# Layer A of a hybrid trunk: longer planned distances in recurrence and merge, four buffers for keys and queries, one decay matrix, f32 gates from the normed tiles, late modulation

## The chip, the cores and the metric

The kernel runs on one core of one Trainium2 chip. Its engines work side by side, each in its own order: TensorE (PE; PEld is its weight load), VectorE (DVE), ScalarE (ACT), GpSimd (POOL) and SyncE (SP), whose queue issues all DMAs here. The metric is the device time of one execution in microseconds, the median of several runs; lower is better.

## The reference

Two layers over 1024 tokens of width 1024, all in f32. Layer A is a gated delta rule with 8 query/key heads and 16 value heads of width 128, layer B an attention with 16 heads of width 64. Each takes `h = rmsnorm(x) * (1 + scale) + shift` and adds `gate * y`; shift, scale and gate come from one conditioning vector times `ada_w`. Layer A, cut to what matters:

```python
proj = h @ w_in                               # q, k, v | z | b, a
qkv = silu(causal_depthwise_conv(qkv, conv_w))
q, k = l2norm(q) * 128**-0.5, l2norm(k)
beta, g = sigmoid(b), -exp(A_log) * softplus(a + dt_bias)
g = cumsum(g)                                 # within a chunk
decay = exp(where(lower, g[:, None] - g[None, :], -inf))
L = where(strict, (beta k) @ k.T * decay, 0); T = inverse(I + L)
u, w = T @ (beta v), T @ (beta k exp(g))
# chunk after chunk:
v_new = u - w @ state
o = (q exp(g)) @ state + (q @ k.T * decay) @ v_new
state = state * exp(g_last) + (k exp(g_last - g)).T @ v_new
o = rmsnorm(o) * silu(z); y = o @ w_out
```

## The kernel before, in words

Large products run as three f32r matmuls over a high and a low part of each operand (`mm3`, L129 issues all matmuls); small ones run in f32. Layer A treats the sequence in two halves of 512 tokens and 8 groups per half (one key head with its two value heads): 16 groups, each with 4 chunks of 128 tokens.

TensorE's order is written out by a planner, `Flow`. Each strand of work is a generator; a step issues some instructions, and its `yield n` says how many planned TensorE nanoseconds must pass before its next step. The planner always takes the ready strand of the best priority; `fill_a` (the projections and then the output projection) has the worst, so its matmuls fill the planned distances. `pst` and `acc_bank` take a PSUM bank out of a ring, `free(bank, n)` plans its return. The distances (`Y_...`, `R_...`, `LAT`) set an order only: at run time TensorE takes its list in order and waits where data is late. The other engines' orders come from the scheduler of the framework, which also places every semaphore.

The strands, per group: `proj_all` projects k, q, two v tiles and z and runs the convolution (ACT, POOL halo copies, three DVE steps of L764). `prepk` makes a decay matrix `d1`, turns k into tokens (`to_tokens`, evicted by ACT, L923) and makes `L` (`lm`). `invert_blocks` inverts 16x16 diagonal blocks on DVE, passing them through DRAM; `LAT` is the planned time from its start to the merge. `invert_merge` builds the full inverse `r` with small matmuls. `prepv` turns v into tokens, `prep2` makes a second decay matrix `d2`, `qd` (q times the decay, on POOL, L950) and the attention matrix `am`. `chain` is the recurrence. For each chunk it uses bank `ch` for k·state (columns 0:256) and `r`·`xp` (columns 256:512), and bank `co` for the output (columns 0:256) and the state's update:

```python
mm(p1[:, 0:256], kf[:, c], st)                            # ch
xp = p1 * weg + uv              # DVE, L978, one head at a time
yield Y_C0
mm(p1[:, 256 + j*P : ...], r[:, j*CPH + c], xp[:, j*P : ...])
vn = copy(p1[:, 256:512])       # ACT, L991
ve = p1[:, 256:512] * ex        # DVE, L992
yield Y_C1
mm(p2, qd, st); mm(p2, am, vn)                            # co
mm(p2[:, 256:512], ktok, ve); st = st * ex + p2           # L1011
yield Y_C2
```

`finish` norms, transposes and stores a group's output. `gates` makes beta and the decays once per half from an own `mm3` tile over 128 columns of which 32 are used. `start_norm` norms the first half and makes the first modulation columns; `next_norm` norms the second half during the first and stores it in DRAM; `ada_all` makes the remaining modulation rows in 16 strips of 256 columns (`ada_strip`, DVE). Layer B follows and is not touched.

Of the kernel before, what the change touches and what calls it, by code (L numbers as in the profile page):

```python
# [15 lines left out]
P = 128  # L16
D = 1024
# [20 lines left out]
Y_PK = 1200  # L38
# [4 lines left out]
Y_P2 = 4000  # L43
Y_MQ = 2500
Y_MR = 3000
Y_M0 = 1900
Y_M1 = 2000
Y_M2 = 2000
Y_M3 = 2000
Y_C0 = 2200  # L50
Y_C1 = 1700
Y_C2 = 2000
Y_F0 = 9000
Y_F1 = 800
Y_F2 = 2550
# [14 lines left out]
LAT = 36000  # L70
# [15 lines left out]
ADP = 2000  # L86
R_AD = 600
R_OA = 1150
# [95 lines left out]
def tile_trunk(  # L184
# [74 lines left out]
    def ada_strip(alloc, palloc, layer, col, width, wtag, atag, btag, ahead, pace):  # L259
# [38 lines left out]
        else:  # L298
# [3 lines left out]
            flow.free(ps, R_AD)  # L302
# [207 lines left out]
    with ExitStack() as sa:  # L510
# [9 lines left out]
        KQ, ZG = 3, 2  # L520
# [4 lines left out]
        neg_a = at([P, 16], "neg_a")  # L525
        xid = at([P, 8, 16], "xid", 1, BF16)
# [18 lines left out]
        def start_norm():  # L545
            xsT = [at([P, HALF], n, b) for n, b in (("k", KQ), ("k", KQ), ("k", KQ), ("q", 2), ("q", 2))]
            xsT += [at([P, HALF], "ktok", 3) for _ in range(3)]
            for t in range(CPH):
                xt = at([P, D], *(("vtok", 3), ("qd", 2))[t // 2])
                nc.sync.dma_start(xt, x[t * P : (t + 1) * P, :])  # L550
                for d in norm_tile(xt, at([P, D], "ogt", 1), lambda k, p, t=t: nc.scalar.copy(
                    xsT[k][:, t * P : (t + 1) * P], p)):
                    flow.t += d
# [11 lines left out]
            for n in range(2):  # L565
                ps = banks[n]
                acc = at([P, D], "d2", 2)
# [15 lines left out]
                if n == 0:  # L583
                    nc.sync.dma_start(bcol, ada_bc)
                    nc.sync.dma_start(norm_c, norm_col)
                    wload()
                    wload()
# [4 lines left out]
            )  # L592
            for k in range(KT):
# [12 lines left out]
            nc.sync.dma_start(dt_b, a_dt.broadcast_to([P, 16]))  # L606
            nc.sync.dma_start(neg_a, a_log.broadcast_to([P, 16]))
# [3 lines left out]
        def norm_tile(xt, jk, evac):  # L611
            rs = rms_rows(xt, jk, at)
            nc.vector.tensor_scalar(xt, xt, rs, None, op0=ALU.mult)
            yield Y_NN
            for k0 in range(0, KT, 4):
# [7 lines left out]
                flow.free(ps, R_N)  # L623
                yield 500

        def next_norm():
            yield from hold(lambda: done["kqv"] >= 2)
            for t in range(CPH):
                tok = CPH * P + t * P
                xt = at([P, D], "nx", 1)  # L630
                if t == 0:
                    nc.vector.tensor_copy(xt[:, 0:KT], ts[0]["gt"]["ngc"][:, 0, 0:KT])
                nc.sync.dma_start(xt, x[tok : tok + P, :])
                yield 4000
                hf = at([P, KT, P], "nh", 1)

                def evac(k, p):
                    nc.vector.tensor_scalar(
                        hf[:, k], p, gcol[0][:, k : k + 1], scol[0][:, k : k + 1],
                        op0=ALU.mult, op1=ALU.add,  # L640
                    )

                yield from norm_tile(xt, hf.rearrange("p k t -> p (k t)"), evac)
                yield 3000
                nc.sync.dma_start(
                    h1_d[:, :, t * P : (t + 1) * P].rearrange("k p t -> p k t"), hf
                )
            done["norm"] = 1

# [10 lines left out]
        def gates(h, gt):  # L660
            wba_h, wba_l, wba_r = (v.rearrange("p (k f) -> p k f", f=P) for v in wtile(D))
            nc.gpsimd.memset(wba_r, 0.0)
            nc.sync.dma_start(wba_r[:, :, 0:32], wa_ba)
            split(wba_h, wba_l, wba_r)
            yield 4000
# [3 lines left out]
            rows = at([P, HALF], "cv_y", 2)[0:32]  # L669
            nc.scalar.copy(rows, ps[0:32])  # L670
            flow.free(ps, R_AD)
            yield 2500
            pc = yield from pst("tr", 2)
            for c in range(CPH):
                tr_(
                    pc[:, c * 32 : c * 32 + 32], rows[:, c * P : (c + 1) * P], ident[0:32, 0:32]
                )
            pv = pc[:, 0 : CPH * 32].rearrange("p (c n) -> p c n", n=32)
# [7 lines left out]
            flow.free(pc, R_N)  # L686
# [18 lines left out]
            nc.scalar.activation(ex, ex, AF.Exp)  # L705
            ngc = at([P, CPH, 16], "g_ngc", 2)
# [12 lines left out]
            gt.update(col=col, ex=ex, ngc=ngc, beta=beta, g_d=g_d)  # L719
# [54 lines left out]
        def proj_all():  # L774
            for i in range(2 * NG):
                h, g = divmod(i, NG)
                if g == 0:
# [11 lines left out]
                    gt = {}  # L789
                    flow.add(gates(h, gt), 1, HC)  # L790
# [6 lines left out]
                yield from hold(lambda: done["prep2"] >= i - 1)  # L797
                t["q"] = qf = at([P, CPH, P], "q", 2)
# [53 lines left out]
        def decay(t, name):  # L852
# [6 lines left out]
            dv = at([P, 2 * CPH, P], name, 2)  # L859
            low = name == "d1"  # L860
            nc.gpsimd.affine_select(
                out=dv, in_=gb.rearrange("p j (c t) -> p (j c) t", t=P),
                compare_op=ALU.is_gt if low else ALU.is_ge, fill=BIG if low else -BIG, base=0,
                pattern=[[0, 2 * CPH], [-1 if low else 1, P]], channel_multiplier=1 if low else -1,
            )
            bias = t["gt"]["col" if low else "ngc"]
            yield Y_DG
            for j in range(2):
                for c in range(CPH):
# [4 lines left out]
                        dv[:, u], dv[:, u], AF.Exp, scale=-1.0 if low else 1.0, bias=bias[:, c, hd : hd + 1]  # L874
                    )
            return gb, dv

        def prepk(t):
            g, gt, kf = t["g"], t["gt"], t["k"]
            _, d1v = yield from decay(t, "d1")  # L880
            yield Y_PK
            t["ktok"] = ktok = at([P, CPH, P], "ktok", 3)
            t["ss"] = ss = at([P, 2, CPH], "gss", 3)
# [3 lines left out]
            nc.vector.tensor_scalar(rk, ss[:, 0], EPS, None, op0=ALU.add)  # L887
            nc.gpsimd.tensor_tensor(rk, rk, mhalf[:, 0:CPH], op=ALU.pow)
            rkb = bc(rk, 2, 2)
            t["un"] = un = at([P, CPH, 2], "un", 3)  # L890
            t["wn"] = wn = at([P, CPH, 2], "wn", 2)
            t["weg"] = weg = at([P, CPH, 2], "weg", 3)
            nc.vector.tensor_tensor(un, gt["beta"][:, :, 2 * g : 2 * g + 2], rkb, op=ALU.mult)
            nc.vector.tensor_tensor(wn, un, rkb, op=ALU.mult)
            nc.vector.scalar_tensor_tensor(
                weg, wn, -1.0, gt["ex"][:, 1, :, 2 * g : 2 * g + 2], op0=ALU.mult, op1=ALU.mult
            )
            t["lm"] = d1v
# [27 lines left out]
        def prepv(t):  # L926
# [4 lines left out]
            for j in range(2):  # L931
                yield Y_PT
                yield from to_tokens(vt[:, j], vtok[:, :, j], None)
# [4 lines left out]
            for c in range(CPH):  # L938
                nc.gpsimd.tensor_tensor(vtok[:, c], vtok[:, c], bc(t["un"][:, c], 2, P), op=ALU.mult)
# [920 lines left out]
```

## Time and profile before

| | us |
|---|---|
| median of 3 runs | 2041.61 (2041.05 to 2041.88) |
| the profiled execution's own time | 2033.73 |
| its span, first to last instruction | 2032.0 |
| PE busy | 1846.4 (91%) |
| PE weight loads | 1539.1 (76%) |
| DVE busy | 1375.5 (68%) |
| ACT busy | 1035.2 (51%) |
| POOL busy | 483.0 (24%) |

Busy time is a union over the span; a wait row names the instruction that waited, what released it, the total, the number of times and the longest. Layer A's projections and recurrence fill the span to about 1100 us, its output projection goes to about 1300, and layer B takes the rest.

### The profile page before, as it was taken

The page shows a single profiled execution, that of the slowest core. Times are in us where ns is not written, and L with a number is a line of the kernel's source. Part 1 is how long each engine was busy: PE and PEld are TensorE (multiplying, and loading weights), DVE is VectorE, ACT ScalarE, POOL GpSimd, SP SyncE. Part 2 cuts the span into 40 slices and gives each one's busy share as a digit, 9 for nine tenths or more (in the row PEclk, how much of TensorE's full clock was granted, in tenths as well). Part 3 has the DMA queues.
Part 4 walks back from the last instruction along what each step waited for, and adds up shares of the span by engine and source line. Part 5 has one row for each costly group of instructions (what it writes and reads, how often), then busy time and mean ns, then how long its engine had stood idle before and what let it go on. Part 6 is the DMA issues. An engine that isn't in the chain of part 4 may idle for free. (4 is left out here: it accounts for less than half of the span.)

```text
span 2032.0 us, 36238 instructions
## 1 busy us (share of the span) xinstructions
PE 1846.4 (91%) x12940; PEld 1539.1 (76%) x12940; DVE 1375.5 (68%) x3319; ACT 1035.2 (51%) x2684; POOL 483.0 (24%) x518
## 2 busy tenths in 40 slices
PE   4878899998998989999989789999999999999898
PEld 3766677777776777777777567789889889889676
DVE  5788888787878566766656467456666666656764
ACT  4555466555545445555444344255655655655631
POOL 2140232221213021222101223331231231331222
PEclk6999899999999999999999899999999999999999
DMA  6686676766656455454469988020110220211523
GB/s 248 229 258 226 219 240 208 227 214 223 187 173 172 127 160 160 155 163 134 134 225 311 328 299 285 23 64 22 63 63 17 68 63 16 65 56 42 167 85 96
DMA packets 235781, 315.72 MB, mean 155 GB/s; under 512 B 103176, under 2 KB 155936, under 8 KB 235600
## 3 DMA queue, kind: packets, MB, share of 16 engines
q1 hardware_dynamic: 235600, 313.41, 47.6%
q8 instruction: 102, 1.67, 0.3%
q14 instruction: 79, 0.65, 0.1%
HBM read 231.67 MB, written 81.67 MB: 154 GB/s over the span
## 5 line engine op out<-in xcount | busy, mean ns | idle before, releaser
L129 PE MATMUL mm<-ht_h,whi 128*128 128x512 f32 x784 | 352.4, 450 | 7.2 <-DVE olo L301 5.6
L129 PE MATMUL mm<-ht_l,whi 128*128 128x512 f32 x784 | 317.5, 405 | 3.9 <-DVE ht_l L601 3.9
L129 PE MATMUL mm<-ht_h,wlo 128*128 128x512 f32 x784 | 318.0, 406 | 1.8 <-POOL wlo L328 1.8
L129 PE MATMUL mm<-whi,h_h 128*128 128x384 f32 x512 | 187.0, 365 | 0.9 <-DVE kn L1449 0.9
L129 PEld LDWEIGHTS mm<-ht_h,whi 128*128 128x128 f32 x784 | 154.6, 197 | 40.1 <-DVE olo L301 6.5
L129 PEld LDWEIGHTS mm<-ht_h,wlo 128*128 128x128 f32 x784 | 153.4, 196 | 37.8 <-POOL wlo L328 2.2
L129 PEld LDWEIGHTS mm<-ht_l,whi 128*128 128x128 f32 x784 | 155.0, 198 | 31.0 <-DVE ht_l L601 5.2
L764 DVE SCALAR_TENSOR_TENSOR cv_y<-cv_t,conv_h,cv_y 128x512 f32<-128x512 f32 x192 | 147.6, 769 | 43.0 <-ACT cv_y L756 40.8
L129 PE MATMUL mm<-whi,h_l 128*128 128x384 f32 x512 | 173.0, 338 | 0.0
L129 PE MATMUL mm<-wlo,h_h 128*128 128x384 f32 x512 | 172.7, 337 | 0.0
L1600 DVE TENSOR_TENSOR ptl<-pt,pth 128x512 fp32r<-128x512 f32 x192 | 106.3, 555 | 93.9 <-ACT pth L1599 92.2
L1599 ACT CAST pth<-pt 128x512 fp32r<-128x512 f32 x192 | 91.1, 476 | 140.0 <-PE pt L133 139.2
L1443 POOL TENSOR_TENSOR rs<-ss,mhalf 128x4 f32<-128x4 f32 x64 | 64.5, 1007 | 332.4 <-DVE ss L1441 326.7
L328 DVE TENSOR_TENSOR wlo<-ht_h,whi 128x512 fp32r<-128x512 f32 x124 | 91.1, 775 | 59.7 <-ACT whi L325 54.7
L1564 ACT ACTIVATE lg<-lg,mx 128x896 f32<-128x896 f32 (+7 forms) x128 | 99.5, 777 | 55.4 <-DVE mx L1556 49.7
L325 ACT CAST whi<-ht_h 128x512 fp32r<-128x512 f32 x124 | 70.7, 618 | 95.8 <-PE mm L129 35.3
L129 PE MATMUL mm<-h_h,whi 128*128 128x512 f32 x240 | 99.9, 416 | 0.7 <-DVE wlo L1699 0.3
L129 PEld LDWEIGHTS mm<-whi,h_h 128*128 128x128 f32 x512 | 97.8, 191 | 3.5 <-ACT v L1445 1.2
L129 PEld LDWEIGHTS mm<-wlo,h_h 128*128 128x128 f32 x512 | 97.4, 190 | 2.0
L133 PE MATMUL pt<-ident,lg 128*128 128x128 f32 (+1 forms) x584 | 95.6, 272 | 2.4 <-ACT lg L1564 2.4
L325 ACT CAST whi<-wlo 128x512 fp32r<-128x512 f32 (+1 forms) x108 | 62.5, 625 | 67.2 <-DMA wlo<-in_wa_c_dram 30.9
L129 PEld LDWEIGHTS mm<-whi,h_l 128*128 128x128 f32 x512 | 96.6, 189 | 0.0
(366 smaller groups left out, 4702.0 us busy)
## 6 DMA issues: line engine op xcount, KB each, us to landing
ht_h<-in_wa_o_dram SPq DMA_DIRECT2D x62, 512.0 KB
wc<-whi SPq DMA_DIRECT2D x45, 512.0 KB
wc<-wlo SPq DMA_DIRECT2D x45, 512.0 KB
wlo<-wc SPq DMA_DIRECT2D x45, 512.0 KB
whi<-wc SPq DMA_DIRECT2D x45, 512.0 KB
wlo<-in_wa_c_dram SPq DMA_DIRECT2D x35, 512.0 KB
oraw<-in_ada_w_dram SPq DMA_DIRECT2D x128, 128.0 KB
gb<-g_d SPq DMA_DIRECT2D x32, 512.0 KB
```

The lines of the kernel that those rows point to most:

```text
L129: self.nc.tensor.matmul(out, lhsT, rhs, start=start, stop=stop)
L133: self.nc.tensor.transpose(out, src, ident)
L325: nc.scalar.copy(hi, src)
L328: (lo_eng or nc.gpsimd).tensor_tensor(lo, src, hi.bitcast(F32), op=ALU.subtract)
L764: nc.vector.scalar_tensor_tensor(y, raw[:, j : j + HALF], w[:, j : j + 1], y, op0=ALU.mult, op1=ALU.add)
L1443: nc.gpsimd.tensor_tensor(rs, ss, mhalf[:, 0:4], op=ALU.pow)
L1564: nc.scalar.activation(lg, lg, AF.Exp, scale=-1.0, bias=mx[:, hh : hh + 1], accum_out=sums[:, tt : tt + 1],)
L1599: nc.scalar.copy(ph_[:, cs], pp[:, cs])
L1600: nc.vector.tensor_tensor(pl_[:, cs], pp[:, cs], ph_[:, cs].bitcast(F32), op=ALU.subtract)
```

## The change

All of it is in layer A.

- Distances: `Y_C0` 2200 to 2700, `Y_C1` 1700 to 2200, `Y_C2` 2000 to 1700, a new `Y_C3` of 1300 ahead of the state's update; merge steps 500 longer each; `LAT` 36000 to 40000.
- `k` has 4 buffers instead of 3 and `q` 4 instead of 2; `q` no longer waits for `prep2`.
- One decay matrix `d2` serves both uses; its upper triangle feeds `L` transposed, so the merge's products are written the other way round. `d1`'s exponentials, `qd`, and the POOL scaling of v go.
- In `chain` the product with `st` takes plain `q`, is written into `ch`, and is scaled on ACT into `qe`; DVE adds `qe` to the output. `vn` is scaled by `wn` in two ACT steps. The v tokens are scaled in their ACT eviction.
- The gates come from f32 products of the normed tiles with 32 columns, inside `start_norm` and `next_norm`.
- `ada_all` starts after the sixth key projection and runs 8 strips of 512 columns in the tiles of `next_norm`.
- `finish` splits and stores one head at a time out of single buffers.

Core of the diff:

```diff
-Y_PK = 1200
+Y_PK = 1000
-Y_P2 = 4000
-Y_MQ = 2500
+Y_P2 = 3000
+Y_MQ = 3000
-Y_M0 = 1900
-Y_M1 = 2000
+Y_M0 = 2400
+Y_M1 = 2500
...
-Y_C0 = 2200
-Y_C1 = 1700
-Y_C2 = 2000
+Y_C0 = 2700
+Y_C1 = 2200
+Y_C2 = 1700
+Y_C3 = 1300
...
-Y_F1 = 800
-Y_F2 = 2550
+Y_F1 = 900
+Y_F2 = 1600
-LAT = 36000
+LAT = 40000
-ADP = 2000
+ADP = 3500
+AD0 = 5
+R_AS = 2500
...
             nc.vector.tensor_copy(b, ps[0:1, 0:width])
-            flow.free(ps, R_AD)
+            flow.free(ps, R_AS)
...
-        KQ, ZG = 3, 2
+        KQ, ZG = 4, 2
...
         def start_norm():
...
+                for t in range(CPH):
+                    mm(
+                        pc[:, t * 32 : t * 32 + 32], xk[:, t * P : (t + 1) * P], wba[:, k],
+                        start=k == 0 and t == 0, stop=k == KT - 1 and t == CPH - 1,
+                    )
                 nc.vector.tensor_tensor(ht_l[:, k], xk, ht_h[:, k].bitcast(F32), op=ALU.subtract)
+            flow.add(gates(0, gts[0], pc[:, 0 : CPH * 32].rearrange("p (c n) -> p c n", n=32), pc), 1, HC)
...
         def next_norm():
...
+                def part(k0):
+                    yield 2000
+                    ps = yield from pst("tr", 2)
+                    for k in range(4):
+                        mm(ps[:, 0:32], hf[0][:, k], wba[:, k0 + k], start=k == 0, stop=k == 3)
...
-        def gates(h, gt):
-            wba_h, wba_l, wba_r = (v.rearrange("p (k f) -> p k f", f=P) for v in wtile(D))
-            nc.gpsimd.memset(wba_r, 0.0)
-            nc.sync.dma_start(wba_r[:, :, 0:32], wa_ba)
-            split(wba_h, wba_l, wba_r)
-            yield 4000
-            ps = yield from acc_bank()
-            for k in range(KT):
-                mm3(ps, wba_h[:, k], wba_l[:, k], ht_h[:, k], ht_l[:, k], k == 0, k == KT - 1)
...
+        def gates(h, gt, pv, bank=None):
...
-                yield from hold(lambda: done["prep2"] >= i - 1)
-                t["q"] = qf = at([P, CPH, P], "q", 2)
+                t["q"] = qf = at([P, CPH, P], "q", KQ)
...
         def prepk(t):
-            _, d1v = yield from decay(t, "d1")
+            t["d2"] = yield from decay(t)
...
+            t["lm"] = lm = at([P, 2 * CPH, P], "d1", 2)
...
                     nc.vector.scalar_tensor_tensor(
-                        d1v[:, u], mq[:, c * P : (c + 1) * P], wn[:, c, j : j + 1], d1v[:, u],
+                        lm[:, u], mq[:, c * P : (c + 1) * P], wn[:, c, j : j + 1], t["d2"][:, u],
...
         def prepv(t):
...
+                for c in (c0, c0 + 1):
+                    o = 2 * (c - c0) * P
+                    nc.scalar.activation(
+                        vtok[:, c].rearrange("p j f -> p (j f)"), tr[:, o : o + 2 * P], AF.Copy,
+                        scale=t["irk"][:, c : c + 1],
+                    )
...
-            for c in range(CPH):
-                nc.gpsimd.tensor_tensor(vtok[:, c], vtok[:, c], bc(t["un"][:, c], 2, P), op=ALU.mult)
...
         def prep2(t):
-            gb, d2 = yield from decay(t, "d2")
-            t["am"] = am = d2.rearrange("p (j c) t -> p j c t", c=CPH)
-            t["qd"] = qd = at([P, 2, CPH, P], "qd", 2)
-            for j in range(2):
-                yield 2 * Y_DX
-                nc.scalar.activation(gb[:, j], gb[:, j], AF.Exp)
-                nc.gpsimd.tensor_tensor(
-                    qd[:, j], qf, gb[:, j].rearrange("p (c t) -> p c t", t=P), op=ALU.mult
-                )
+            t["am"] = am = t["d2"].rearrange("p (j c) t -> p j c t", c=CPH)
...
         def chain(t):
...
-                            xt[:, sl], p1[:, sl], weg[:, c, j : j + 1], uv[:, c, j],
+                            xt[:, sl], p1[:, sl], neg[:, c, 2 * g + j : 2 * g + j + 1], uv[:, c, j],
...
-                nc.scalar.copy(vn, p1[:, 256:512])
+                for j in range(2):
+                    nc.scalar.activation(
+                        vn[:, j * P : (j + 1) * P], p1[:, 256 + j * P : 256 + (j + 1) * P], AF.Copy,
+                        scale=wn[:, c, j : j + 1],
+                    )
                 nc.vector.tensor_tensor(
                     ve, p1[:, 256:512].rearrange("p (j f) -> p j f", f=P),
-                    bc(ex[:, 0, c, 2 * g : 2 * g + 2], 2, P), op=ALU.mult,
+                    bc(wex[:, c], 2, P), op=ALU.mult,
                 )
-                flow.free(p1, R_C)
+                if not first:
+                    mm(p1[:, 0:256], qf[:, c], st)
+                    qe = at([P, 2 * P], "qe", 2)
+                    for j in range(2):
+                        sl = slice(j * P, (j + 1) * P)
+                        nc.scalar.activation(
+                            qe[:, sl], p1[:, sl], AF.Copy, scale=ex[:, 1, c, 2 * g + j : 2 * g + j + 1]
+                        )
+                flow.free(p1, R_C + 1000)
                 yield Y_C1
                 p2 = yield from pst("co", 1)
                 for j in range(2):
                     sl = slice(j * P, (j + 1) * P)
-                    if not first:
-                        mm(p2[:, sl], qd[:, j, c], st[:, sl], start=True, stop=False)
-                    mm(p2[:, sl], am[:, j, c], vn[:, sl], start=first, stop=True)
+                    mm(p2[:, sl], am[:, j, c], vn[:, sl])
+                yield Y_C3
                 mm(p2[:, 256:512], ktok[:, c], ve.rearrange("p j f -> p (j f)"))
...
+                oc = og[:, c].rearrange("p j f -> p (j f)")
+                if first:
+                    nc.scalar.copy(oc, p2[:, 0:256])
+                else:
+                    nc.vector.tensor_tensor(oc, p2[:, 0:256], qe, op=ALU.add)
                 for j in range(2):
                     jk = at([P, P], "sqt", 1, BF16)
-                    nc.scalar.activation(
-                        jk, p2[:, j * P : (j + 1) * P], AF.Square, accum_out=so[:, c, j : j + 1]
-                    )
-                nc.scalar.copy(og[:, c].rearrange("p j f -> p (j f)"), p2[:, 0:256])
+                    nc.scalar.activation(jk, og[:, c, j], AF.Square, accum_out=so[:, c, j : j + 1])
...
         def finish(t, og, so):
...
+                ogh, ogl = at([P, HALF], "ogh", 1, F32R), at([P, HALF], "ogl", 1, F32R)
+                split(ogh, ogl, ogt, lo_eng=nc.vector)
+                yield Y_F2
+                for v, d in ((ogh, og_d), (ogl, ogl_d)):
+                    nc.sync.dma_start(d[2 * g + j, :, h * HALF : (h + 1) * HALF], v.bitcast(F32))
...
         def ada_all():
-            yield from hold(lambda: done["gates"] == 1)
+            yield from hold(lambda: done["kp"] >= AD0 + 1)
...
             for l, cl in strips:
-                for w0 in (0, 256):
-                    yield from ada_strip(
-                        xt_, acc_bank, l, cl + w0, 256, ("oraw", 3), ("ohi", 4), ("olo", 4), 1, ADP
-                    )
+                yield from ada_strip(
+                    al, acc_bank, l, cl, 512, ("nx", 2), ("nh", 2), ("nh", 2), 1, ADP
+                )
```

More of the change, by code (lines that the diff above doesn't have):

```diff
@@ L592, in start_norm @@
             )
+            pc = yield from pst("tr", 2)
             for k in range(KT):
@@ L623, in norm_tile, with xload @@
                 flow.free(ps, R_N)
+                if part is not None:
+                    yield from part(k0)
                 yield 500
+        gts = [{}, {}]
         def next_norm():
             yield from hold(lambda: done["kqv"] >= 2)
-            for t in range(CPH):
[L629 to L633, printed above, removed]
-                yield 4000
-                hf = at([P, KT, P], "nh", 1)
+            xts = []
+            def xload(t):
+                tok = CPH * P + t * P
+                xts.append(at([P, D], "nx", 2))
+                if t < 2:
+                    nc.vector.tensor_copy(xts[t][:, 0:KT], ts[0]["gt"]["ngc"][:, 0, 0:KT])
+                nc.sync.dma_start(xts[t], x[tok : tok + P, :])
+            xload(0)
+            yield 6000
+            for t in range(CPH):
+                xt = xts[t]
+                if t < CPH - 1:
+                    xload(t + 1)
+                hf = []
@@ L644, in next_norm @@
+                yield from norm_tile(xt, None, evac, part)
                 yield 3000
-                nc.sync.dma_start(
-                    h1_d[:, :, t * P : (t + 1) * P].rearrange("k p t -> p k t"), hf
-                )
             done["norm"] = 1
+            flow.add(gates(1, gts[1], gin), 1, HC)
         def load_norm():
@@ L685, in gates @@
             nc.scalar.activation(e, e, AF.Exp, scale=-1.0)
-            flow.free(pc, R_N)
+            if bank is not None:
+                flow.free(bank, R_N)
             nc.vector.tensor_scalar(beta, beta, 1.0, None, op0=ALU.add)
@@ L788, in proj_all @@
                         load_norm()
-                    gt = {}
-                    flow.add(gates(h, gt), 1, HC)
+                    gt = gts[h]
                 t = dict(h=h, g=g, gt=gt)
@@ L930, in prepv @@
             vtok = at([P, CPH, 2, P], "vtok", 3)
-            for j in range(2):
+            for c0 in range(0, CPH, 2):
                 yield Y_PT
-                yield from to_tokens(vt[:, j], vtok[:, :, j], None)
+                tr = yield from pst("tr", 2)
+                for c in (c0, c0 + 1):
+                    for j in range(2):
+                        o = (2 * (c - c0) + j) * P
+                        tr_(tr[:, o : o + P], vt[:, j, c], ident)
+                for c in (c0, c0 + 1):
+                    o = 2 * (c - c0) * P
[3 more added lines that the diff above has]
+                    )
+                flow.free(tr, R_T)
             done["tr"] += 1
@@ L963, in chain @@
             h, g, gt, kf, r = t["h"], t["g"], t["gt"], t["k"], t["r"]
-            ktok, qd, am, uv, weg, epo, ex = t["ktok"], t["qd"], t["am"], t["uv"], t["weg"], t["epo"], gt["ex"]
+            ktok, qf, am, uv, epo, ex = t["ktok"], t["q"], t["am"], t["uv"], t["epo"], gt["ex"]
+            wn, wex, neg = t["wn"], t["wex"], gt["neg"]
             st = state[g]
```

160 lines of the change are left out of this document (78 added, 82 removed).

## The prediction

> **What bounds the kernel now.** I read the busy time by stage first, then TensorE's waits in the longest stage, then the order of time around one wait.
>
> Columns of the first rows: stretch, its length, then busy time of PE, PE's weight loads, DVE, ACT and POOL, the granted clock, the DMA share and GB/s.
>
> ```profile
> span 2032.0 us, 36238 instructions
> 0.00:50.00 50.00, 22.63 (x100) 19.76 (x100) 29.23 (x44) 20.90 (x56) 13.50 (x29) 0.70 0.69 252
> 50.00:1100.00 1050.00, 946.42 (x8070) 768.86 (x8071) 779.30 (x1952) 551.01 (x1631) 217.68 (x279) 0.95 0.62 195
> 1100.00:1300.00 200.00, 174.08 (x764) 138.15 (x763) 124.90 (x226) 81.32 (x157) 64.14 (x50) 0.95 0.77 265
> PE co L129 <- DVE ve L992: 19.6, 15, 2.3
> PE tr L133 <- ACT vtok L923: 16.0, 5, 7.0
> PE ch L129 <- DVE xp L978: 11.5, 7, 2.6
> PE su L129 <- DMA rmat<-rb: 11.1, 2, 9.5
> PE co L129 <- ACT vn L991: 7.1, 7, 2.8
> PE tr L133 <- ACT ktok L923: 6.0, 1, 6.0
> PE mm L129 <- DVE olo L301: 5.6, 3, 2.4
> ```
>
> Nearly all of layer A, and everything the diff touches, lies in 0 to 1300. From 50 to 1100 (projections with the recurrence) TensorE is busy 946.4 of 1050 us; no other engine passes 779.3 (DVE), and DMA is at 0.62. So this stretch lasts as long as TensorE's work, its idle time (103.6 us) and what it loses at a lower clock. The wait rows (total, times, longest) give 76.9 of the 103.6; the other rows of that view are under 3.5 each. Layer B, the 732 us behind it, is not changed.
>
> An idle stretch is paid more than once, as the matmul starts around one show:
>
> ```profile
> 882.02 0.39 PE L129 MATMUL mm<-ht_l,whi 128*128 128x512 f32 x1
> 882.24 0.39 PE L129 MATMUL mm<-ht_h,wlo 128*128 128x512 f32 x1
> 896.73 0.66 PE L133 MATMUL tr<-ident,vt 128*128 128x128 f32 x4 [2.24 <-ACT vtok L923]
> 897.62 0.63 PE L129 MATMUL mm<-ht_l,whi 128*128 128x512 f32 x1
> 898.05 0.63 PE L129 MATMUL mm<-ht_h,wlo 128*128 128x512 f32 x1
> ```
>
> The same 128x512 matmul starts every 0.22 us before the 2.24 us gap and every 0.43 after it: half rate. The granted clock of the stretch is 0.95, so some 52 us of full clock are missing over 1050 us, against 103.6 us idle; part of those 52 falls into the idle time itself. I charge 0.4 us for each idle us (range 0.2 to 0.5). The Trainium skill (TensorE: Matmul & The Clock Gate, The HAM clock gate) puts the return to half rate after an idle window of about 3.4 us; the gap above is shorter and was followed by it, so the trace decides. By that rule the clock terms below, those gained and those lost, would be near nothing.
>
> **The change, part by part.**
>
> *Recurrence.* In each of 56 chunks (8 groups, 8 chunks each, without the first of each group) the product of the query with the state leaves bank `co`, where it was two 128-column products of `qd`, and becomes one 256-column product of `q`, written into columns 0:256 of bank `ch`. In the program it stands right behind the products `r`·`xp` and behind the three reads of columns 256:512 of the same bank, `vn` (twice now) and `ve`, with nothing planned between. What happens when TensorE writes a bank whose other columns are still being read? These rows are the nearest:
>
> ```profile
> 836.49 0.34 DVE L978 SCALAR_TENSOR_TENSOR xp<-ch,weg,vtok 128x128 f32<-128x128 f32 x1
> 837.74 0.34 DVE L978 SCALAR_TENSOR_TENSOR xp<-ch,weg,vtok 128x128 f32<-128x128 f32 x1
> 838.13 0.71 PE L129 MATMUL ch<-xp,rmat 128*128 128x128 f32 x4 [0.75 <-DVE xp L978]
> DVE ve L992 <- ACT vn L991: 10.3, 12, 3.0
> ```
>
> The first of the four matmuls at 838.13 needs only the first half of `xp`, finished at 836.83, and writes columns 256:384. It starts at 838.13, just after the second half's instruction (837.74 + 0.34 = 838.08) has read columns 128:256 of that bank, and TensorE had been idle 0.75 us. And `ve` waits for `vn` (12 times, 10.3 us), though both only read the bank. So this program puts accesses of two engines to one bank in order whatever their columns. The Trainium skill (PSUM — Partial Sum Buffer, PSUM bank collisions raise a hardware error) asks for just that: guard by bank and 32-partition quadrant, since a write against a read of other columns collides too.
>
> So the new product waits until `ve` is read, and everything behind it on TensorE, the projection matmuls that now fill this time, waits too. The price is the time from the end of `r`·`xp` to the end of `ve`, which today is covered:
>
> ```profile
> L129 PE MATMUL ch<-xp,rmat x4: 270/274/275, 904.8 to 905.1; 128*128 128x128 f32 x4
> 905.41 0.37 ACT L991 COPY vn<-ch 128x256 f32<-128x256 f32 x1 [0.74 <-PE ch L129]
> 905.82 0.42 DVE L992 TENSOR_TENSOR ve<-ch,g_ex 128x256 f32<-128x256 f32 x1 [0.42 <-ACT vn L991]
> 727.53 0.60 PE L129 MATMUL ch<-xp,rmat 128*128 128x128 f32 x4
> 729.78 1.56 ACT L873 ACTIVATE d<-d,g_ngc 128x128 f32<-128x128 f32 x5
> 731.24 0.36 ACT L991 COPY vn<-ch 128x256 f32<-128x256 f32 x1
> 734.37 0.42 DVE L992 TENSOR_TENSOR ve<-ch,g_ex 128x256 f32<-128x256 f32 x1
> L992 DVE TENSOR_TENSOR ve<-ch,g_ex x64: 405/418/426, 184.2 to 1099.3; 128x256 f32<-128x256 f32 x64
> ```
>
> The quick case: last `r`·`xp` start 905.1 + 0.27, `ve` ends 905.82 + 0.42 = 906.24: 0.87 us. The slowest: 728.13 (727.53 + 0.60) to 734.79: 6.66. Over the 64 pairs (first and last start in the row of `ve`) the mean is 2.4, the median 2.0. `vn` gets a second instruction, scaled from a column:
>
> ```profile
> L991 ACT COPY vn<-ch 128x256 f32<-128x256 f32 x64 | 24.0, 374 | 36.8 <-PE ch L129 36.6
> L756 ACT ACTIVATE cv_y<-mm,conv_h 128x512 f32<-128x512 f32 x64 | 44.4, 694 | 0.0
> L755 ACT COPY cv_t<-mm 128x512 f32<-128x512 f32 x64 | 37.4, 584 | 27.8 <-PE mm L129 27.6
> L873 ACT ACTIVATE d<-d,g_gc 128x128 f32<-128x128 f32 x128 | 39.2, 389 | 22.6 <-POOL d L861 13.7 <-POOL cv_t L759 8.9
> L764 DVE SCALAR_TENSOR_TENSOR cv_y<-cv_t,conv_h,cv_y 128x512 f32<-128x512 f32 x192 | 147.6, 769 | 43.0 <-ACT cv_y L756 40.8 <-ACT qq L1129 0.4
> L949 ACT ACTIVATE gb<-gb 128x512 f32<-128x512 f32 x32 | 18.4, 618 | 0.0
> L1020 ACT COPY og<-co 128x256 f32<-128x256 f32 x64 | 23.3, 364 | 0.0
> L950 POOL TENSOR_TENSOR qd<-q,gb 128x512 f32<-128x512 f32 x32 | 43.1, 1368 | 27.4 <-ACT gb L949 19.1 <-DVE q L771 4.8 <-DVE rk L887 3.5
> L939 POOL TENSOR_TENSOR vtok<-vtok,un 128x256 f32<-128x256 f32 x64 | 44.8, 730 | 78.6 <-ACT vtok L923 71.3 <-DVE xi L1090 7.4
> L129 PE MATMUL co<-state,qd 128*128 128x128 f32 x220 | 43.9, 282 | 0.0
> L129 PE MATMUL ch<-state,k 128*128 128x256 f32 x112 | 34.4, 389 | 2.0 <-DVE state L1011 1.3 <-DVE ln_ss L308 0.6
> ```
>
> A column scale costs 694 − 584 = 110 ns over the plain copy; five 128-wide exponentials ran in 1.56 us, 0.31 each, so two scaled halves take 0.39 + 0.31 = 0.70 in place of 0.37: +0.33. The stall is then between 0.87 + 0.33 = 1.2 and 2.4 + 0.33 = 2.7 us per chunk. I take 2.1, since some of what stood ahead goes (next paragraph): 56 × 2.1 = 118 us, × 1.4 for the clock = 165 us. Bounds: 56 × 1.2 × 1.2 = 81 and 56 × 2.7 × 1.5 = 227.
>
> *Other engines.* ACT loses one set of exponentials (`d1`, 39.2 us), those of `gb` (18.4) and the copy to `og` (64 × 0.364 = 23); it gains the halves of `vn` (64 × 0.33 = 21), `qe` (56 × 0.70 = 39) and the scaled `vtok` copies (4 × 0.48 in place of 2 × 0.59 per group, 12 over 16 groups): about −9 us, but the burst ahead of `vn` at 729.78 gets shorter. POOL loses `qd` (43.1) and the scaling of `vtok` (44.8), 88 us, and half of its selects, none of it on TensorE's path. DVE gains the sum `p2` + `qe` (56 × 0.42 = 23) and loses about as much in the modulation strips (half as many instructions of twice the width): even. These only shorten queues; I have put that into 2.1 instead of 2.7.
>
> *TensorE's own work.* 43.9 us of `qd` products give way to 34.4 us like the `k` row: −9.5. The gates lose 48 projection matmuls (× 0.226 = 11) and gain 64 f32 products of 32 columns, which the trace records as two each: 128 × 0.20 (43.9 / 220 in the row above) = 25 at most; they are a quarter as wide, so I take 16, with 11 as the lower end. Net −4.5 (bounds −9 to +5). In the first half they stand ahead of the first projection tile, which now waits for the whole normed half: up to 24 × 0.226 = 5.4 us later, but the separate gates tile of the same length is gone: 0.
>
> *Waits that go.* Behind the new stall `vn` and `ve` are always ready: 7.1 + 19.6 = 26.7 us gone, whatever the planned distances. Of the other 76.9 us: `xp` (mean 1.6, 0.5 more distance) −6; `rmat` (40 instead of 36 planned, a fourth `k` and `q` buffer as filler) −9 of 11.1; `vtok` and `ktok` (22) half, −11, as their queues shorten while TensorE stands; `olo` (four evictions of doubled width with four times the distance) −5; the small rows, 27 us, −9. That is 66.7 us, × 1.4 = 93. At most all 103.6 × 1.5 = 155 go.
>
> *Stores and loads.* `finish` now holds one head's split in a single buffer, so the second head's cast waits until the first is stored. The nearest row is a cast-like ACT step that waited for a store out of a single buffer:
>
> ```profile
> ACT nh L307 <- DMA h_d<-nh: 5.8, 2, 5.6
> ```
>
> 16 × 2.9 = 46 us of ACT at most, nothing at least; ACT is half idle, TensorE pays when `vn` or `vtok` stands behind: +8 taken (0 to 30). The modulation weights move from the first to later groups, and 16 of 32 `gb` loads (8 MB) go; with DMA at 0.62 I give that nothing. From 1100 to 1300 (DMA 0.77, TensorE idle 26 us) a slower layer A lets the output weights arrive earlier: −8 (0 to −20). The start gets to the gates 12 us sooner (planned waits of 4.0 and 2.5 us and a tile of 24 × 0.226 fall away) and 4 later to the merge: −8, which the fourth buffer's term already holds, so 0.
>
> **Sum**: +165 − 93 − 4.5 + 8 − 8 = +67. The other terms being as likely larger (once TensorE stands 118 us more, the queues behind the remaining 37 us of waits drain also: −15 × 1.4 = −21), I forecast **+46 us**: 2033.7 us was the profiled execution's own time (span 2032.0), so about 2080 there; the median of the runs is 7.9 us above it, hence **2088 us**.
>
> **The rivals.** *The stall is there but smaller than what it buys* (faster). The place is the same; the price is 56 × 1.4 × 1.2 = 94 us, if `ve` and `vn` come near their quick case, and the gains 140 of the 155, − 4.5. −50 us: 1991. It decides when the stall is under some 1.7 us with 80% of the old waits gone. For it: a fifth of the 64 pairs lie under 1.1 us. Against it: `ve` stands in DVE's order behind 770 ns convolution steps, and those stay.
>
> *No stall at all*, the write being let through beside reads of other columns: gains 93 to 155, + 4.5, −8: about −115: 1927. Against it stands the row at 838.13.
>
> *The edits cancel* to within 4 us: 2042. About 0.2% is what a measurement of this kernel can tell from no change.
>
> *Worse than the sum*: nothing of the queues drains, 2.7 us per chunk, and ACT's wait for the stores: +130 to +150: 2180. It is the upper end of the forecast's own range.
>
> **How the numbers follow.** Forecast and its upper end 0.60, smaller stall 0.28, no stall 0.07, cancelling 0.05. Faster 0.35, same 0.05, slower 0.60. The forecast's own range is 2050 to 2165. The range for 8 in 10 reaches into the faster case: 1980 to 2165; below it lie the case without a stall and a little of the smaller stall, above it the worst.
>
> **What would show it.** Right: in TensorE's waits a row `ch` behind DVE `ve` with some 56 entries, 100 us or more, first in that view; `co` behind `ve` and `vn` gone; a granted clock from 50 to 1100 of 0.93 or less, with this stretch near 1100 us long in place of 1050; `co<-state,qd` gone and a `ch<-state,q` row near 34 us. Wrong: the product of `q` and the state starting while `vn` or `ve` still read the bank, or its wait under 1.2 us on average; or the old waits shrinking by over 100 us. The wait of `rmat` behind its load (11.1 us) should nearly go in any case, and a new row of ACT `ogh` behind the store of `ogh` would show the single buffer.

## The result

The changed kernel takes 2122.45 us (median of 4 runs, 2118.31 to 2126.87), the kernel before, on the same chip, 2041.74: 1.0395 times as long, 95% interval 1.0373 to 1.0418. The change costs 81 us. The forecast was 2088 us, with 2050 to 2165 as its own range.

The stretches of the profiled execution after (span 2122.0 us). The cut behind the projections stands at 1180, 80 us later than in the rows of before: the last projection matmul ends at 1125.4 (1035.8 before), and the recurrence runs on beside the output projection to 1228 (1103 before). Columns as in the rows of before: length, busy time of PE, PE's weight loads, DVE, ACT, POOL, granted clock, DMA share, GB/s.

```profile
0.00:50.00 50.00, 23.32 (x105) 21.21 (x105) 30.67 (x48) 22.12 (x59) 10.31 (x27) 0.69 0.69 262
50.00:1180.00 1130.00, 972.46 (x7940) 787.10 (x7941) 736.63 (x1925) 541.10 (x1587) 102.21 (x165) 0.93 0.53 169
1180.00:1390.00 210.00, 186.15 (x833) 149.69 (x832) 133.18 (x251) 89.72 (x188) 65.22 (x49) 0.97 0.80 275
1390.00:2122.00 732.00, 703.78 (x4018) 613.74 (x4016) 443.02 (x1099) 382.81 (x842) 189.36 (x162) 0.99 0.19 62
```

The last 732 us, layer B, are as before. The stretch with the projections is 1130 us long in place of 1050, at a granted clock of 0.93 in place of 0.95. DVE and POOL do less than before (736.6 and 102.2 us busy against 779.3 and 217.7), ACT as much. TensorE's waits from 50 to 1190 (total, times, longest):

```profile
PE ch L132 <- DVE ve L1022: 106.8, 54, 4.3
PE ch L132 <- DVE state L1048: 16.5, 8, 3.8
PE tr L136 <- ACT vtok L964: 6.8, 3, 4.5
PE ch L132 <- DVE xp L1004: 5.8, 8, 1.6
PE ch L132 <- DVE state L1046: 5.5, 3, 3.2
...
PE co L132 <- ACT vn L1018: 1.0, 1, 1.0
```

The first row was not there before (to 1180 it holds 53 waits, 104.0 us); `co` behind `ve` (19.6) is gone and `co` behind `vn` has gone from 7.1 to 1.0. Over the whole of layer A the groups of the two products with the state read so, count, busy time and mean ns, then TensorE's idle time ahead of them:

```profile
L132 PE MATMUL ch<-state,q 128*128 128x256 f32 x112 | 44.9, 487 | 111.5 <-DVE ve L1022 111.5
L132 PE MATMUL ch<-state,k 128*128 128x256 f32 x112 | 36.7, 410 | 23.2 <-DVE state L1048 16.5 <-DVE state L1046 5.5 <-DVE xtmp L1120 1.1
```

111.5 us of idle time stand ahead of the 56 products (recorded as 112), 1.99 us for each. One of them in order of time, TensorE, then ACT, then DVE:

```profile
1037.35 0.60 PE L132 MATMUL ch<-xp,rmat 128*128 128x128 f32 x4
1039.13 0.70 PE L132 MATMUL ch<-state,q 128*128 128x256 f32 x2 [1.18 <-DVE ve L1022]
1039.48 0.58 PE L132 MATMUL mm<-ht_h,whi 128*128 128x512 f32 x1
1037.99 0.63 ACT L1018 ACTIVATE vn<-ch,wn 128x128 f32<-128x128 f32 x2
1038.65 0.42 DVE L1022 TENSOR_TENSOR ve<-ch,wex 128x256 f32<-128x256 f32 x1
```

The last `r`·`xp` matmul ends at 1037.95. The two halves of `vn` run 1037.99 to 1038.62, `ve` 1038.65 to 1039.07, and the product starts at 1039.13, after 1.18 us of idle TensorE. ACT and DVE were free here, so this is the floor, the shortest that this wait gets (19 of the 56 took 1.17 or 1.18 us); the projection matmul at 1039.48 had nothing to wait for but its place in the order.

### The profile page after: what moved, and what is told of

It reads as the page before. It is cut to its first block, busy times and chain, and to the rows that moved or that the text cites. A ratio compares the mean times of both kernels' runs of the same rounds, so it can differ in the third digit from the quotient of the medians.

```text
span 2122.0 us, 35794 instructions
## 1 busy us (share of the span) xinstructions
PE 1885.7 (89%) x12892; PEld 1571.7 (74%) x12892; DVE 1343.5 (63%) x3321; ACT 1035.7 (49%) x2672; POOL 367.1 (17%) x402
## 5 line engine op out<-in xcount | busy, mean ns | idle before, releaser
L132 PE MATMUL mm<-ht_h,whi 128*128 128x512 f32 x768 | 356.8, 465 | 0.2 <-ACT cv_y L784 0.2
L132 PE MATMUL ch<-state,q 128*128 128x256 f32 x112 | 44.9, 487 | 111.5 <-DVE ve L1022 111.5
L132 PEld LDWEIGHTS ch<-state,q 128*128 128x128 f32 x112 | 18.6, 208 | 122.2 <-DVE ve L1022 122.2
L136 PE MATMUL pt<-ident,lg 128*128 128x128 f32 (+1 forms) x584 | 95.6, 272 | 3.1 <-ACT lg L1601 3.1
```

Of the source, the lines that this page charges most:

```text
L132: self.nc.tensor.matmul(out, lhsT, rhs, start=start, stop=stop)
L136: self.nc.tensor.transpose(out, src, ident)
```

## The experiments

All times below are medians; ratios are to the kernel before on the same chip. The runs are from several chips, so kernels are compared by their ratios, and a gain or loss in us between two kernels is the difference of their ratios times 2041.74. My theory: the product of q and the state stands behind three reads of its own bank, the program orders accesses of different engines to one bank, and the wait itself, with TensorE's half rate behind it, is the loss. The rivals: the other edits cost the time; or the product waits for its place or its data, not for the bank.

### The product ahead of the reads

```diff
+                if not first:
+                    mm(p1[:, 0:256], qf[:, c], st)
                 vn = at([P, 2 * P], "vn", 2)
...
                 if not first:
-                    mm(p1[:, 0:256], qf[:, c], st)
                     qe = at([P, 2 * P], "qe", 2)
```

> The changed kernel with the product of q and the state issued right behind r·xp, ahead of the reads vn and ve; qe stays behind them. Same work, same bank. My theory (the product waits for the three reads of its bank): the wait of 106.8 us behind ve in the changed kernel from 50 to 1180 goes, with some 0.45 us of clock for each idle us, and some 15 us come back where co waits for vn and ve as before: 2122 - 107 × 1.45 + 15, about 1980 (1950 to 2010). Rival (the loss comes from the other edits, the longer distances, the single store buffers or the heavier DVE path from the state, and TensorE would only wait elsewhere): not under 2080.

Measured: 1982.67 us, ratio 0.9741 (0.971 to 0.9772): by the ratios 134 us less than the changed kernel, by moving one matmul up by three instructions. TensorE's largest waits in its layer A, now 1234 us long:

```profile
PE ch L132 <- DVE state L1049: 19.6, 11, 4.4
PE mm L132 <- DVE d L579: 13.4, 2, 9.1
PE tr L136 <- DVE vtok L629: 8.4, 1, 8.4
PE tr L136 <- ACT vtok L964: 8.0, 3, 5.7
PE ch L132 <- DVE state L1047: 7.6, 3, 3.6
```

No row of `ch` behind `ve` is left, and none of `co` behind `ve`; `co` behind `vn` is 0.8 us. The theory holds, the first rival falls: all other edits are in this kernel, and it is faster than the kernel before.

### The product in another bank

```diff
+                pq = None if first else (yield from pst("tr", 2))
                 for j in range(2):
                     mm(
                         p1[:, 256 + j * P : 256 + (j + 1) * P], r[:, j * CPH + c],
...
-                    mm(p1[:, 0:256], qf[:, c], st)
+                    mm(pq[:, 0:256], qf[:, c], st)
...
-                            qe[:, sl], p1[:, sl], AF.Copy, scale=...
+                            qe[:, sl], pq[:, sl], AF.Copy, scale=...
+                    flow.free(pq, R_C + 1000)
-                flow.free(p1, R_C + 1000)
+                flow.free(p1, R_C)
```

> The changed kernel with the product of q and the state at its place behind vn and ve, but written into a bank of the ring tr instead of columns 0:256 of ch; qe reads it there. My theory (order by bank): no wait of the product for ve, since nothing else reads that bank; about 1985 (1950 to 2030, the tr ring being fuller). Rival (the product waits for its place in the order, or for the state, whatever the bank): the wait behind ve stays near 100 us and the time near 2120.

Measured: 1986.01 us, ratio 0.9753 (0.9719 to 0.9788). The product keeps its place behind `vn` and `ve`, and its row reads

```profile
L132 PE MATMUL tr<-state,q 128*128 128x256 f32 x112 | 34.3, 389 | 3.4 <-DVE ogt L1088 1.6 <-ACT rmat L1173 1.6 <-ACT ktok L947 0.2
```

3.4 us of idle time in place of 111.5, none of it behind `ve`. So it is the bank, not the place in the order and not the state. The Trainium skill (PSUM — Partial Sum Buffer, PSUM bank collisions raise a hardware error) asks for guards by bank and 32-partition quadrant, not by address; the columns 0:256 and 256:512 of this case were kept apart in time just so, and a second bank freed them.

### This part alone, in the kernel before

In the room of `qd`, `q` gets a third buffer here and no longer waits for `prep2`. `vn` stays one plain copy, so two reads stand ahead of the product, not three.

```diff
-            t["qd"] = qd = at([P, 2, CPH, P], "qd", 2)
...
-                flow.free(p1, R_C)
+                if not first:
+                    mm(p1[:, 0:256], qf[:, c], st)
+                    qe = at([P, 2 * P], "qe", 2)
+                    ...
+                flow.free(p1, R_C + 1000)
...
-                    if not first:
-                        mm(p2[:, sl], qd[:, j, c], st[:, sl], start=True, stop=False)
-                    mm(p2[:, sl], am[:, j, c], vn[:, sl], start=first, stop=True)
+                    mm(p2[:, sl], am[:, j, c], vn[:, sl])
...
+                    nc.vector.tensor_tensor(oc, p2[:, 0:256], qe, op=ALU.add)
```

> The kernel before with this one part of the change: the product of q and the state behind vn and ve in bank ch, scaled into qe, added on DVE; qd and its exponentials are gone, all else (two decay matrices, distances, late or early modulation, gates) is as before. My theory: the stall alone, at least 0.87 us in each of 56 chunks and near 2.2 on average, 120 us × 1.45, less the 26.7 us × 1.45 of co waits and 9.5 us of TensorE work: about 2041 + 125, 2165 (2120 to 2200), slower than the whole change, whose other parts gain. Rival (the other parts cost, the product is cheap): 2030 to 2060.

Measured: 2153.52 us, ratio 1.0575 (1.052 to 1.063), the slowest of all.

```profile
PE ch L129 <- DVE ve L984: 108.7, 56, 6.6
PE ch L129 <- DVE xp L970: 14.7, 11, 5.6
```

The same wait, 56 times, 108.7 us. And with the product ahead of the reads:

```diff
+                if not first:
+                    mm(p1[:, 0:256], qf[:, c], st)
                 vn = at([P, 2 * P], "vn", 2)
```

> The kernel of e3_alone (the kernel before with the product of q and the state in bank ch) with that product ahead of the reads vn and ve. Theory (in e3_alone only the stall was bad, and the rest of the change gains on its own): the wait behind ve of 102.6 us goes, the co waits of the kernel before return: 2035 to 2050, ratio 1.000 within 0.010, as the product saves 9.5 us of TensorE work and loads DVE by 23. Rival (moving this product off qd and POOL is itself what makes the changed kernel with the early product fast): ratio 0.985 or less.

Measured: 2037.04 us, ratio 0.9979 (0.996 to 0.9999). The wait is gone (the waits of `co` are back, 18.9 us behind `ve` and 5.3 behind `vn`), and what remains of this part is worth next to nothing: as theory had it. Put together:

| ratio to before | qd as before | product ahead of the reads | product behind the reads |
|---|---|---|---|
| rest as before | 1 | 0.998 | 1.058 |
| rest as changed | not run | 0.974 | 1.040 |

The place of one matmul is worth 6.0% (1.058 / 0.998) and 6.7% (1.040 / 0.974); the rest of the change gains some 2.4% (0.974 / 0.998) with the product ahead of the reads, and 1.7% (1.040 / 1.058) with it behind them.

### The product behind a planned distance

```diff
-                if not first:
+                yield Y_C1
+                if not first:
                     mm(p1[:, 0:256], qf[:, c], st)
...
                 flow.free(p1, R_C + 1000)
-                yield Y_C1
```

> The changed kernel with the product of q and the state (and qe) moved behind the planned distance Y_C1, same bank: 2.2 us of planned work now stand between r·xp and it. My theory: only the part of each wait over that distance is left, 20 to 35 us where 106.8 were: 2122 - 80 × 1.45, about 2005 (1970 to 2040). Rival (the other edits cost): not under 2080.

Measured: 1996.54 us, ratio 0.981 (0.9776 to 0.9844).

```profile
PE ch L132 <- DVE ve L1022: 12.8, 13, 2.4
```

12.8 us are left of it, less than the 20 to 35 I expected. The order by bank is still there, but now 2.2 us of planned work stand ahead of the product and cover most of the wait.

### Which of the other parts gain

With the product ahead of the reads, the old planned distances:

```diff
-Y_C0 = 2700
-Y_C1 = 2200
-Y_C2 = 1700
-Y_C3 = 1300
-LAT = 40000
+Y_C0 = 2200
+Y_C1 = 1700
+Y_C2 = 2000
+Y_C3 = 0
+LAT = 36000
...
```

> The kernel of e1_first (product of q and the state ahead of the reads) with the old planned distances in recurrence, merge and inversion (2200, 1700, 2000, none ahead of the state's update; merge 2500, 1900, 2000; 36000; 1200 and 4000 in prepk and prep2); all else as changed. Theory one (the longer distances carry the gain that e1_first has over the kernel before, 0.974): most of it is lost, ratio 0.99 to 1.00, with co waiting for ve and vn by some 25 us again and rmat behind its load by some 10. Theory two (the gain comes from less work on the other engines, one decay matrix, no qd and no scaling on POOL): ratio 0.97 to 0.985.

Measured: 1977.15 us, ratio 0.9688 (0.965 to 0.9727): not slower at all. Theory one, that the longer distances carry the gain, falls; the ratio is a little under theory two's range. The waits moved:

```profile
PE co L132 <- DVE ve L1024: 18.3, 12, 2.8
PE co L132 <- ACT vn L1020: 5.0, 5, 1.8
PE ch L132 <- DVE state L1047: 2.5, 1, 2.5
PE ch L132 <- DVE state L1049: 1.2, 1, 1.2
```

23.3 us at `co` are back, and the 27.2 us for the state (19.6 + 7.6 in the rows of the kernel with the new distances) have shrunk to 3.7. I ran both once more on one chip:

> The kernel of e1_first once more beside the next two, on one chip. Expected: ratio 0.974 within 0.004.

> The kernel of f1_dist once more beside e1_first. Theory (longer distances move waits from co to the state's return and gain nothing in sum): ratio 0.969 within 0.004, at or under e1_first's. Rival (chip to chip difference): at or over e1_first's.

0.9719 (0.9692 to 0.9746) with the new distances and 0.9687 (0.9658 to 0.9716) with the old: no difference that these runs can tell. A mixture, with only `Y_C1` and `Y_C3` as long as in the change and the others old:

```diff
-Y_C1 = 1700
-Y_C3 = 0
+Y_C1 = 2200
+Y_C3 = 1300
```

> The kernel of f1_dist with only the distances ahead of vn and ve longer (Y_C1 2200, Y_C3 1300). f1_dist waits 23.3 us at co and 3.7 us for the state. Theory (a longer recurrence only moves the wait): the co waits fall to under 8, the state's or others rise by half of it, ratio 0.966 to 0.974. Rival (these two are the useful distances): ratio 0.960 or less.

Measured: 0.9708 (0.9685 to 0.9732). Again no difference that these runs can tell. And a longer `Y_C2`, against the wait for the state:

```diff
-Y_C2 = 1700
+Y_C2 = 2800
```

> The kernel of e1_first with 2800 instead of 1700 ns planned between the state's update and the next chunk (Y_C2). e1_first waits 27.2 us there for the state on DVE. Theory (that wait is filled by projection work): 27 falls to under 10, ratio 0.960 to 0.968. Rival (the recurrence gets too long for its filler, or the wait moves): 0.972 or more.

Measured: 2007.64 us, ratio 0.985 (0.9825 to 0.9875), slower than the kernel it was made from (0.9741).

```profile
PE mm L132 <- DMA ohi<-og_d: 10.4, 11, 3.3
PE tr L136 <- DVE vt L799: 9.0, 4, 3.6
PE ch L132 <- DVE state L1049: 7.3, 7, 2.8
PE ch L132 <- DVE state L1047: 7.1, 4, 4.1
```

The wait for the state did fall, from 27.2 to 14.4 us, not under 10, but the transposes of v (9.0 after 4.2) and the output projection's loads (10.4 after 5.3) wait more. The rival had it right; why the whole is some 22 us longer (0.985 against 0.974) isn't settled by these rows.

Three buffers for keys and queries in place of four:

```diff
-        KQ, ZG = 4, 2
+        KQ, ZG = 3, 2
```

> The kernel of e1_first with three buffers for keys and queries in place of four. Theory (the fourth buffer gives filler while the first inversion is under way): the wait of rmat behind its load near 150 us comes back with some 10 us, ratio 0.978 to 0.985 where e1_first had 0.974. Rival (filler is there anyway): 0.974 within 0.003.

Measured: 2023.45 us, ratio 0.9923 (0.9897 to 0.9949). So taking the fourth buffer out of the full set costs 1.8%, more than I expected and most of the 2.4% that the rest gains. The fourth buffer alone, in the kernel before, was not run.

```profile
PE su L132 <- DVE tmat L1148: 13.3, 4, 7.7
PE mm L132 <- DMA ohi<-og_d: 13.2, 7, 5.1
PE ch L132 <- DVE xp L1004: 9.1, 6, 2.8
```

The longest wait, 7.7 us, ends at 246 us: the merge waits for a transpose on DVE (L1148), and that for the load `rmat<-rb`. This is the theory's kind of wait, in a later merge than the one near 150 us that I had named. A second one of 5.1 us stands at 734; the rest is spread (`xp` 9.1 after 4.0).

Last, the changed kernel itself, stalled product and all, with two of its distances back:

```diff
-Y_C1 = 2200
-Y_C3 = 1300
+Y_C1 = 1700
+Y_C3 = 0
```

> The changed kernel, product of q left where it waits, with Y_C1 back at 1700 and Y_C3 at 0. Theory (behind the stall vn and ve are always ready, so these two distances hide nothing there): the time of the changed kernel within 10 us, ratio 1.035 to 1.045, and no co wait for ve. Rival (they hide part of it): 1.05 or more, with co waits of 15 us or more.

Measured: 2118.97 us, ratio 1.0394 (1.0365 to 1.0423), equal to the changed kernel. `ch` waits 124.8 us behind `ve`, 13 more than in the changed kernel, and 9.6 us for the state where that has 22.0; `co` waits 2.4 us for `ve`. Behind the stall these distances hide nothing in sum.

## Why the prediction was right, point by point

*Where the time went.* Layer A up to layer B's first matmul, in the kernel before, in the changed kernel, and in the changed kernel with the product ahead of the reads:

```profile
0.00:1281.00 1281.00, 1125.06 (x8824) 909.34 (x8825) 921.66 (x2184) 646.53 (x1826) 280.61 (x341) 0.94 0.65 210
```

```profile
0.00:1373.00 1373.00, 1165.86 (x8779) 942.29 (x8780) 889.59 (x2187) 646.60 (x1815) 165.02 (x226) 0.92 0.58 190
```

```profile
0.00:1234.00 1234.00, 1122.29 (x8776) 909.91 (x8777) 880.30 (x2186) 641.96 (x1814) 171.06 (x225) 0.95 0.64 211
```

From the first row to the second, idle TensorE rose from 1281 − 1125.1 = 155.9 to 1373 − 1165.9 = 207.1 us: +51. Busy TensorE rose by 41 although its instructions are 45 fewer. Together these are the 92 us that the two stretches differ by. Most of the 41 is the clock: by the traces' records of the granted clock, TensorE was busy at half clock for 111.9 us before and 180.0 after, and 68 us more at half clock cost 34.

The third row splits the 92. The stall, with all that follows from it, costs 1373 − 1234 = 139 us; the rest of the change gains 1281 − 1234 = 47 (each row is one profiled execution; by the ratios of the medians it is 134 and 53). In the forecast's own terms the stall was 165 − 21 = 144 (the −21 for the queues that drain while TensorE stands belongs to it), and the rest was −93 − 4.5 + 8 − 8 = −97.5. So the mechanism and the price of the stall were right. The term that was mis-sized is the gain of the waits that go, about twice what came, and this is why +46 became +81 (+90 between the two profiled executions).

*The stall.* Forecast 56 × 2.1 = 118 us, between a floor of 1.2 and 2.7 for each. Measured 111.5, 1.99 for each, floor 1.18. The row at 838.13 that carried it was only a near case; the run in another bank shows the order by bank directly.

*The clock.* I charged 0.4 us for each idle us. For the stall this was about right: between the third and the second row idle TensorE rises by 207.1 − 111.7 = 95.4 us and busy TensorE by 43.6, 0.46 for each idle us. For the waits that go it was not: between the first row and the third idle TensorE falls by 44.2 us and busy TensorE by only 2.8. One reason is the start, where the first long period at half clock lasts 47.8 us in place of 37.5 and costs some 5 us; the rest is open. What a gap does to the rate shows in the starts behind it:

```profile
799.38 0.70 PE L132 MATMUL ch<-state,q 128*128 128x256 f32 x2 [2.09 <-DVE ve L1022]
799.73 0.58 PE L132 MATMUL mm<-ht_h,whi 128*128 128x512 f32 x1
800.15 0.40 PE L132 MATMUL mm<-ht_l,whi 128*128 128x512 f32 x1
800.37 0.60 PE L132 MATMUL mm<-ht_h,wlo 128*128 128x512 f32 x1
800.77 0.63 PE L132 MATMUL mm<-ht_h,whi 128*128 128x512 f32 x1
801.20 0.63 PE L132 MATMUL mm<-ht_l,whi 128*128 128x512 f32 x1
801.62 0.63 PE L132 MATMUL mm<-ht_h,wlo 128*128 128x512 f32 x1
```

The gap is 2.09 us long; 1 us later the starts are 0.43 us apart, for some 3 us. After the 1.18 us gap at 1039.13 they are 0.23 apart, all but the first. Of the 56 stalls, the 30 under 1.8 us saw a half-clock record begin in the gap or within 3.4 us behind it once, the 19 from 1.8 to 3.4 us 14 times, and the 7 longer ones each time. So not every short stall costs clock; those near 2 us mostly do. The Trainium skill (TensorE: Matmul & The Clock Gate, The HAM clock gate) names an idle window of about 3.4 us; gaps well under that were mostly followed by half rate here, so the rule as an upper limit for harmless gaps doesn't hold in this kernel.

*Waits that go.* Forecast 66.7 us of idle time, then 15 more as queues drain. Without the stall's own row, layer A is idle for 207.1 − 111.5 = 95.6 us, against 155.9 before: 60 gone, not 82. Of these some 16 go with the stall (111.7 idle without it), which are the 15 of the queues; the other 44 stand against 66.7. In the stretches of the waits it is 1130 − 972.5 − 104.0 = 53.5 against 103.6. `vtok` (16.0 to 6.8), `xp` (11.5 to 5.8), `rmat` and `olo` (gone from the rows) went as said. `co` behind `ve` and `vn` went also, but the longer distances do that without a stall: with the product ahead of the reads 0.8 us is left. What was missing is a new wait, `k`·state behind the state on DVE, 16.5 + 5.5 us where 1.3 stood, and 27.2 with the product ahead of the reads; I had put it at nothing. The shorter `Y_C2` is one part of it, since a longer one halved it; but with the same `Y_C2` and a shorter `Y_C1` and `Y_C3` it was 9.6 us, so it isn't shown to be all.

*TensorE's own work.* Forecast −9.5 for the product and +5 for the gates. Before and after, the products in question:

```profile
L129 PE MATMUL co<-state,qd 128*128 128x128 f32 x224 | 44.7, 282 | 0.0
```

```profile
L132 PE MATMUL tr<-wba,nh 128*128 128x32 f32 x64 | 9.9, 291 | 4.4 <-DVE nh L668 4.4
L132 PE MATMUL tr<-wba,k 128*128 128x32 f32 x24 | 5.5, 403 | 5.1 <-ACT k L607 3.2 <-DVE k L609 1.9
L132 PE MATMUL tr<-wba,ktok 128*128 128x32 f32 x24 | 5.3, 401 | 0.0
L132 PE MATMUL tr<-wba,q 128*128 128x32 f32 x16 | 3.6, 401 | 0.0
```

The product takes 44.9 us as it stands, no less than `qd`'s 44.7, since it comes right after a wait and partly at half rate; ahead of the reads it takes 35.0, the saving that was forecast, so the stall ate it:

```profile
L132 PE MATMUL ch<-state,q 128*128 128x256 f32 x112 | 35.0, 395 | 0.0
```

The gates' narrow products take 24.3 us, the upper end of 11 to 25. Those of the first half (`k`, `ktok`, `q`) take 401 to 403 ns each, twice the 200 I had reckoned with: they run from 44.9 to 61.7 us, while the granted clock is at one half.

*Stores.* The single buffer shows up as forecast, small (ACT's idle time ahead of `ogh`, total and times); what TensorE pays for it no run separates:

```profile
  DMA og_d<-ogh: 12.7, 6
```

*The rivals.* For a stall that buys more than it costs I had named 1.7 us each. With what was measured the bound is lower: 139 us for 111.5 us of stall is 1.25 for each us, and gains of 47 us pay for 47 / 1.25 / 56 = 0.7 us each (0.8 by the ratios), less than the floor of 1.18. So this case was out of reach. No stall at all is ruled out for this kernel. That planned distances hide nothing behind the stall was right; without the stall they gain nothing either, in sum.

## What to carry to other kernels

Before writing into the free columns of a PSUM bank, list who still reads the other columns: in this kernel the write waited for all of them, and everything behind it in TensorE's order waited too. Issue such a product ahead of the reads, give it another bank, or put filler between: the three gave back 134, 131 and 119 us here. When a bundle of edits comes out slow, its largest new wait row shows which one to move, and the rest may be a gain. When forecasting such a bundle, look for the waits that the new order creates as well as for those that it ends.

## What the runs showed that I had not expected

Lengthening planned distances only moved TensorE's waits: 23.3 us at `co` against 27.2 us for the state, at the same time for both, and 1100 ns more in one place cost 1% (0.985 against 0.974). One more buffer for keys and queries, which I had counted for some 9 us, is worth about 37 (1.8%) in the full set. And a run of the kernel that keeps all edits but moves one matmul is 2.6% faster than the kernel before, 1982.67 us; with the old distances it reached 1974 to 1977, the fastest of these.
